# Norms of a two-block transformer kernel: 1/sqrt by a polynomial and one Newton step, VectorE's next 40 operations ordered behind it, and a ring of four for four wide weights

## The chip, the core and the metric

The kernel runs on one core of one Trainium2 chip. The metric is the device time of one execution in microseconds, as the median of several. A core has a matrix engine (TensorE, PE in the rows, with its weight load PEld), a vector engine (VectorE, DVE), an activation engine (ScalarE, ACT), a general engine (GpSimd, POOL) and a queue that starts transfers (SyncE, SP). Each engine works through its own row of instructions in a fixed order and waits where an operand is not there yet.

## What is computed

The reference is two blocks after one another over 512 tokens of width 1024. In the first, layer 0 is a mixer (chunked mLSTM beside a gated short convolution) and layer 1 grouped-query attention, with a context of 256 tokens beside; both have a squared-relu MLP. In the second, both layers add three branches (a latent attention "MLA", a differential attention with 8 heads, a memory attention), then a layer norm, an MLP and another layer norm. What matters here is where an inverse root is taken:

```python
def rms_norm(x, g):
    xf = x.astype(jnp.float32)
    y = xf * lax.rsqrt(jnp.mean(xf * xf, axis=-1, keepdims=True) + EPS)
    return (y * g.astype(jnp.float32)).astype(x.dtype)

def _layernorm(x, g, b):
    mu = jnp.mean(xf, axis=-1, keepdims=True)
    var = jnp.mean(jnp.square(xf - mu), axis=-1, keepdims=True)
    y = (xf - mu) * lax.rsqrt(var + LN_EPS) * g.astype(jnp.float32) + b.astype(jnp.float32)
    return y.astype(x.dtype)

# first block, both layers
hx = rms_norm(x, norm1_g[layer]) * (1 + mod_x[1]) + mod_x[0]
...
x = x + mod_x[5] * sqrelu_mlp(rms_norm(x, norm2_g[layer]) * (1 + mod_x[4]) + mod_x[3], mlp_w1[layer], mlp_w2[layer])
# mixer: hn = rms_norm(h, mnorm_g), attention: rms_norm of q and k by head, MLA: _rms(c_q), _rms(c_kv),
# differential attention: _rms by head of the output, second block: _layernorm after the branches and after the MLP
```

## The kernel before

**Matmuls.** Every product is taken as three: both operands are split into a high part and a remainder (`split`, L546 and L547: ScalarE casts `whi` or `Hh`, VectorE or GpSimd subtracts to get `wlo` or `Hl`), and TensorE adds high times high, high times low and low times high (L528; L531 are transposes). 512 tokens go in two parts of 256 where a norm lies between, and whole where none does.

**Weights.** They stream in one fixed order (`weight_order`) through a ring of four raw tiles, started by SyncE, and are split into rings of high and low tiles. One subtraction in three goes to GpSimd, in some stretches one in two or none. Weights of 1056 columns, which are the mixer's four `hv` pieces, have a ring of their own, `vh` and `vl`, with two tiles each. The two-tile ring is line 582.

**Norms.** The squares are summed by VectorE over the blocks of rows (`accx`, L349, for the x side), TensorE sums over the partitions with a product with ones (`colsum`), VectorE makes the variance (`var`, L737, L422 or L2139) and calls `rsqrt` (L711 to L726): a shift (L719), the well-known integer guess (L720), a product with -0.5 (L721) and three Newton steps of three operations (L723 to L725), 12 small operations on 128 x 2 to 128 x 12 numbers, of which each but one needs the one before. TensorE then spreads the result over the partitions (`bcast`, a product with the constant `cst`), and the apply step multiplies (L364). In the attention and the differential attention the result is used per head (`rq`, and `rsy` for the head outputs). There are 54 calls: 2 at the start, 6 in the mixer, 3 in the output projection of the mixer, 3 in the MLP's second product of layer 0, 2 for keys and 8 for queries in the attention, 2 in its output projection, and in each layer of the second block 2 in the MLA, 8 in the differential attention and 4 in the layer norms.

**Order.** The program is written as generators that take turns; a scheduler then fixes each engine's row from the order of emission, the dependences and its own estimate of durations. It is free to put an operation that was emitted later between two operations of an `rsqrt` chain, and does: operations such as `junk` (L636, the adaptive norms' modulations as a fused multiply and sum over a raw weight tile), `wlo`, `r` (L822, the squared relu) and the rotary steps (L1337 to L1340, with one step, `rp`, on GpSimd) stand between the chains' operations. Where the words say "a chain", they mean one `rsqrt` call's operations.

**Places named below.** In the mixer the product `px` takes its four `vh`/`vl` pieces in turn; the same stretch multiplies `Hch`, the context's high part, with `whi` into `pc`. In the output projection of the mixer each of three parts ends with four `accx` additions, `colsum` and `bcast`. In the differential attention each head transposes its probabilities `P` (L531), ScalarE casts them to `pth`, VectorE makes the remainder `ptl` (L547), and the head's next keys `dk` and queries `dq` pass the rotary steps.

## Time and profile before

| | before |
|---|---|
| median of 3 runs | 3865.19 us (3862.13 to 3867.59) |
| profiled execution | 3866.64 us |
| its span | 3864.8 us, mean granted clock 0.979 |
| TensorE busy | 3684.8 us (95%) |
| VectorE busy | 2450.4 us (63%) |
| ScalarE busy | 1560.9 us (40%) |
| GpSimd busy | 843.3 us (22%) |

The span is the time from the profile's first to its last instruction; the execution's own time is 1.8 us longer. The times of single operations below are of this execution. TensorE is busy in nearly all of it, so a time is told by where it is not busy: its waits, each with what ended it, and the stretches in which its granted clock was 0.5 and every product took twice as long.

### The profile page before, as it was taken

The page shows a single profiled execution, that of the slowest core. Times are in us where ns is not written, and L with a number is a line of the kernel's source. Part 1 is how long each engine was busy: PE and PEld are TensorE (multiplying, and loading weights), DVE is VectorE, ACT ScalarE, POOL GpSimd, SP SyncE. Part 2 cuts the span into 40 slices and gives each one's busy share as a digit, 9 for nine tenths or more (in the row PEclk, how much of TensorE's full clock was granted, in tenths as well). Part 3 has the DMA queues.
Part 4 walks back from the last instruction along what each step waited for, and adds up shares of the span by engine and source line. Part 5 has one row for each costly group of instructions (what it writes and reads, how often), then busy time and mean ns, then how long its engine had stood idle before and what let it go on. Part 6 is the DMA issues. An engine that isn't in the chain of part 4 may idle for free.

```text
span 3864.8 us, 52371 instructions
## 1 busy us (share of the span) xinstructions
PE 3684.8 (95%) x20472; PEld 3175.4 (82%) x20472; DVE 2450.4 (63%) x4615; ACT 1560.9 (40%) x2822; POOL 843.3 (22%) x550
## 2 busy tenths in 40 slices
PE   7999999999988999999999999999999999999998
PEld 7877888888878888888888778888878887788887
DVE  7577575544588784456667866544676678555445
ACT  5222432222447643335544543422365445334222
POOL 3112210000120121112222224211333222242112
PEclk8999999999989999999999999999999999999999
DMA  7322233331210133322122122222121211123331
GB/s 280 126 88 95 91 128 135 126 124 64 70 55 7 55 106 104 94 77 72 67 73 71 50 63 102 90 96 98 58 76 66 78 66 50 64 95 93 95 97 44
DMA packets 94359, 337.11 MB, mean 87 GB/s; under 512 B 10272, under 2 KB 15008, under 8 KB 93216
## 3 DMA queue, kind: packets, MB, share of 16 engines
q1 hardware_dynamic: 94112, 333.77, 25.5%
q8 instruction: 161, 2.64, 0.3%
q14 instruction: 86, 0.70, 0.1%
HBM read 326.39 MB, written 7.34 MB: 86 GB/s over the span
## 4 chain that ended last, share of the span: by engine, by line
PE 71%; DVE 11%; ACT 4%; issue 2%; POOL 2%; POOLq 0%; ACTq 0%; DVEq 0%
PE b L528 63%; PE d L528 6%; PE b L531 2%; DVE rr L1340 1%; DVE ptl L547 1%; ACT P L1315 1%; DVE wlo L547 1%; DVE nm L1307 1%; DVE rp L1337 1%; POOL mg L1681 1%; POOL rp L1339 0%; DVE dq L1599 0%; DVE rsq L723 0%; DVE qo L1599 0%; DVE rp L1338 0%
## 5 line engine op out<-in xcount | busy, mean ns | idle before, releaser
L546 ACT CAST whi<-raw 128x1024 fp32r<-128x1024 f32 (+1 forms) x349 | 363.5, 1042 | 821.7 <-PE b L528 544.0
L528 PE MATMUL b<-Hl,whi 128*128 128x512 f32 (+1 forms) x1456 | 547.2, 376 | 5.8 <-POOL Hl L547 5.0
L528 PE MATMUL b<-Hh,whi 128*128 128x512 f32 (+1 forms) x1456 | 547.5, 377 | 4.8 <-ACT Hh L546 3.5
L528 PE MATMUL b<-Hh,wlo 128*128 128x512 f32 (+1 forms) x1456 | 544.7, 375 | 0.8 <-DVE wlo L547 0.8
L547 POOL TENSOR_TENSOR wlo<-raw,whi 128x1024 fp32r<-128x1024 f32 (+1 forms) x115 | 280.4, 2438 | 1018.7 <-ACT whi L546 986.1
L547 DVE TENSOR_TENSOR wlo<-raw,whi 128x1024 fp32r<-128x1024 f32 (+1 forms) x234 | 313.6, 1340 | 217.4 <-ACT whi L546 214.6
L528 PEld LDWEIGHTS b<-Hl,whi 128*128 128x128 f32 x1456 | 276.0, 190 | 54.8 <-POOL Hl L547 8.4
L528 PEld LDWEIGHTS b<-Hh,whi 128*128 128x128 f32 x1456 | 275.4, 190 | 51.8 <-ACT Hh L546 4.4
L528 PEld LDWEIGHTS b<-Hh,wlo 128*128 128x128 f32 x1456 | 276.1, 190 | 50.3 <-DVE wlo L547 1.0
L546 ACT CAST xhi<-raw 128x1024 fp32r<-128x1024 f32 x145 | 151.7, 1049 | 391.9 <-PE b L528 383.9
L547 POOL TENSOR_TENSOR xlo<-raw,xhi 128x1024 fp32r<-128x1024 f32 x50 | 122.5, 2450 | 782.3 <-ACT xhi L546 756.1
L822 DVE TENSOR_TENSOR r<-r 128x512 f32<-128x512 f32 (+1 forms) x176 | 176.6, 1018 | 128.1 <-ACT r L821 127.9
L528 PE MATMUL b<-Hl,xhi 128*128 128x512 f32 (+1 forms) x624 | 228.6, 367 | 1.1 <-POOL Hl L547 1.0
L528 PE MATMUL b<-Hh,xhi 128*128 128x512 f32 (+1 forms) x624 | 227.0, 365 | 2.2 <-ACT Hh L546 2.2
L528 PE MATMUL b<-Hh,xlo 128*128 128x512 f32 (+1 forms) x624 | 227.1, 364 | 0.0
L636 DVE SCALAR_TENSOR_TENSOR junk<-raw,sc 128x1024 bf16<-128x1024 f32 x128 | 161.6, 1263 | 91.8 <-DMA raw<-in_wts 90.7
L531 PE MATMUL b<-cst,P 128*128 128x128 f32 x960 | 149.8, 281 | 50.8 <-DVE ptl L547 25.3
L528 PE MATMUL b<-hlx,xhi 128*128 128x512 f32 (+1 forms) x532 | 196.3, 369 | 0.0
L528 PE MATMUL b<-hhx,xlo 128*128 128x512 f32 (+1 forms) x532 | 196.2, 369 | 0.0
L528 PE MATMUL b<-hhx,xhi 128*128 128x512 f32 (+1 forms) x532 | 195.7, 368 | 0.0
L547 DVE TENSOR_TENSOR ptl<-b,pth 128x512 fp32r<-128x512 f32 (+1 forms) x272 | 165.9, 621 | 32.5 <-ACT pth L546 30.2
L528 PE MATMUL b<-hlx,whi 128*128 128x512 f32 (+1 forms) x504 | 185.8, 369 | 0.0
(669 smaller groups left out, 9726.8 us busy)
## 6 DMA issues: line engine op xcount, KB each, us to landing
raw<-in_wts SPq DMA_DIRECT2D x566, 512.0 KB, 3.4
early<-in_wts SPq DMA_DIRECT2D x16, 512.0 KB, 7.7
raw<-in_wts SPq DMA_DIRECT2D x6, 384.0 KB, 3.0
raw<-in_wts SPq DMA_DIRECT2D x4, 528.0 KB, 3.9
x<-in_xT SPq DMA_DIRECT2D x2, 1024.0 KB, 10.7
X<-in_xT SPq DMA_DIRECT2D x1, 2048.0 KB, 9.2
xd<-X SPq DMA_DIRECT2D x2, 1024.0 KB, 5.4
X<-xd SPq DMA_DIRECT2D x1, 2048.0 KB, 7.8
```

Of the source, the lines that this page charges most:

```text
L528: self.nc.tensor.matmul(out, lhsT=lhsT, rhs=rhs, start=start, stop=stop, skip_group_check=True)
L531: self.nc.tensor.transpose(out, in_, ident)
L546: nc.scalar.copy(out=hi, in_=src)
L547: (eng or nc.vector).tensor_tensor(out=lo, in0=src, in1=hi.bitcast(F32), op=ALU.subtract)
L636: nc.vector.scalar_tensor_tensor(out=junk, in0=w[:, :1024], scalar=0.5, in1=self.sc[:, v, :], op0=ALU.mult, op1=ALU.mult, accum_out=self.m ...
L822: nc.vector.tensor_tensor(out=r, in0=r, in1=r, op=ALU.mult)
L1307: nc.vector.tensor_reduce(out=nm[:, 0:1], in_=S, axis=AX.XY if len(S.shape) == 3 else AX.X, op=ALU.max, negate=True)
L1315: nc.scalar.activation(out=out, in_=S, func=AF.Exp, bias=b, scale=scale, accum_out=ssum)
L1337: nc.vector.stream_shuffle(out=t2, in_=ps, mask=mask)
L1340: nc.vector.tensor_tensor(out=dst, in0=t1, in1=t2, op=ALU.add)
L1681: nc.gpsimd.tensor_tensor(out=X[:, b, :], in0=H[0][:, b, :].bitcast(F32), in1=H[1][:, b, :].bitcast(F32), op=ALU.add)
```

## The change

`rsqrt` has 8 operations where it had 12: the guess in one operation (integer multiply by -0.5 and add of a constant), a quadratic polynomial of x = v g g in four, and one Newton step in three; all eight depend on one another in a row. `pin` then takes the next 40 VectorE operations that are emitted after a chain and gives each an order-only dependence on the chain's last operation (no semaphore), so that the scheduler cannot place them ahead of it or within it. In the layer norm the small product `lne` that follows the chain belongs to it. The mixer's wide ring has four tiles of `vh` and `vl` where it had two, and to pay for it the six row tiles of the mLSTM lie in a pool that is opened later (`rows2`).

```diff
@@ Norm.stats (layer norm)
         r = k.rsqrt(v, n)
+        k.pinned = None
         nc.vector.scalar_tensor_tensor(out=e, in0=d[:, :n], scalar=-1.0 / 1024, in1=r, op0=ALU.mult, op1=ALU.mult)
+        k.pin(True)
@@ _split
-            hi, lo = (self.t(self.wide, [P, 1152], F32R, tag=f"v{x}", bufs=2)[:, :1056] for x in "hl")
+            hi, lo = (self.t(self.wide, [P, 1152], F32R, tag=f"v{x}", bufs=4)[:, :1056] for x in "hl")
@@ rsqrt
-        nc.vector.tensor_scalar(out=i, in0=v.bitcast(I32), scalar1=1, scalar2=None, op0=ALU.logical_shift_right)
-        nc.vector.tensor_scalar(out=y.bitcast(I32), in0=i, scalar1=-1.0, scalar2=float(0x5F3759DF), op0=ALU.mult, op1=ALU.add)
-        nc.vector.tensor_scalar(out=h, in0=v, scalar1=-0.5, scalar2=None, op0=ALU.mult)
-        for _ in range(3):
-            nc.vector.tensor_tensor(out=q, in0=y, in1=y, op=ALU.mult)
-            nc.vector.tensor_tensor(out=q, in0=q, in1=h, op=ALU.mult)
-            nc.vector.scalar_tensor_tensor(out=y, in0=q, scalar=1.5, in1=y, op0=ALU.add, op1=ALU.mult)
+        self.pin(None)
+        nc.vector.tensor_scalar(out=g.bitcast(I32), in0=v.bitcast(I32), scalar1=-0.5, scalar2=float(0x5F374800), op0=ALU.mult, op1=ALU.add)
+        k, a, b = 0.37587863, -1.25284868, 1.87697019
+        r = k ** 0.5
+        nc.vector.scalar_tensor_tensor(out=q, in0=g, scalar=r, in1=g, op0=ALU.mult, op1=ALU.mult)
+        nc.vector.tensor_tensor(out=x, in0=q, in1=v, op=ALU.mult)
+        nc.vector.scalar_tensor_tensor(out=x, in0=x, scalar=a / r, in1=x, op0=ALU.add, op1=ALU.mult)
+        nc.vector.scalar_tensor_tensor(out=g, in0=x, scalar=b, in1=g, op0=ALU.add, op1=ALU.mult)
+        nc.vector.scalar_tensor_tensor(out=q, in0=g, scalar=-0.5, in1=g, op0=ALU.mult, op1=ALU.mult)
+        nc.vector.tensor_tensor(out=q, in0=q, in1=v, op=ALU.mult)
+        i = nc.vector.scalar_tensor_tensor(out=y, in0=q, scalar=1.5, in1=g, op0=ALU.add, op1=ALU.mult)
+        self.pin(i)
         return y
+    PIN = 40
+    def pin(self, ins):
+        tr = self.nc.cur_bb.bb.instructions
+        last = getattr(self, "pinned", None)
+        if last is not None:
+            a, pos = last
+            n = 0
+            for o in tr[pos:]:
+                if o.engine == a.engine and n < self.PIN:
+                    n += 1
+                    self.tc.add_manual_dep(o, a.name, mybir.DependencyInfo(mybir.DependencyClass.NoSync, mybir.DependencyReason.DATA), reason="order")
+        self.pinned = None
+        if ins is not None and self.PIN:
+            a = tr[-1]
+            self.pinned = (a, len(tr))
@@ mlstm
-        row = lambda tag: self.t(rp, [R, TA], tag=tag)
+        rq = self.pool(e_rows, "rows2")
+        row = lambda tag: self.t(rq, [R, TA], tag=tag)
```

The scheduler's rows change with it, far beyond the lines of the diff. Three places follow, each before and after. The lines of the changed kernel are shifted by 2 (split) to 27 (the branches).

ScalarE's row in the mixer, where the four wide weights `vh` are cast; `whi` are narrower weights, `q`, `k`, `va` and `ktm` copies of products. Before:

```order
L546 CAST whi_971<-raw_846 128x1024
L546 CAST vh_1089<-raw_911 128x1056
L546 CAST vh_1149<-raw_969 128x1056
L546 CAST whi_1029<-raw_864 128x1024
L1066 ACTIVATE q_893<-pc_917 128x256
L1066 ACTIVATE q_893<-px_918 128x512
L546 CAST whi_1359<-raw_1147 128x1024
```

and, ten copies of `va` and `ktm` further on:

```order
L1083 COPY ktm_896<-ms_1315 128x256
L546 CAST vh_1155<-raw_1027 128x1056
L1076 COPY va_895<-px_1319 128x2x128
L1083 COPY ktm_896<-ms_1347 128x256
L546 CAST vh_1353<-raw_1087 128x1056
L1076 COPY va_895<-px_1363 128x2x128
```

After:

```order
L548 CAST whi_963<-raw_838 128x1024
L548 CAST vh_1081<-raw_903 128x1056
L548 CAST vh_1141<-raw_961 128x1056
L548 CAST vh_1147<-raw_1019 128x1056
L548 CAST whi_1021<-raw_856 128x1024
L1092 ACTIVATE q_885<-pc_909 128x256
L1092 ACTIVATE q_885<-px_910 128x512
L548 CAST vh_1345<-raw_1079 128x1056
L548 CAST whi_1351<-raw_1139 128x1024
L1092 ACTIVATE q_885<-pc_967 128x256
```

The third cast of `vh` stands right behind the second and the fourth between two copies of q; before, they stood among the copies of `va` and `ktm`.

VectorE's row at the end of the mixer's output projection, before. `X` is the residual after its last product, `accx` the sum of squares, `hlc` and `r` belong to the context's MLP, the `rs` names to the chain:

```order
L1003 SCALAR_TENSOR_TENSOR X_3546<-b_723_4297,mods_69,X_3546 128x256
L636 SCALAR_TENSOR_TENSOR junk_4853,mods_69<-raw_4403,sc_95 128x1024
L547 TENSOR_TENSOR Hl_86<-tmp_4200,Hh_85 128x256
L349 TENSOR_TENSOR accx_3622<-accx_3622,tmp_4236 128x256
L636 SCALAR_TENSOR_TENSOR junk_4855,mods_69<-raw_4403,sc_95 128x1024
L349 TENSOR_TENSOR accx_3622<-accx_3622,tmp_4265 128x256
L822 TENSOR_TENSOR r_4446<-r_4446 128x256
L349 TENSOR_TENSOR accx_3622<-accx_3622,tmp_4294 128x256
L349 TENSOR_TENSOR accx_3622<-accx_3622,tmp_4323 128x256
L547 TENSOR_TENSOR hlc_4394<-r_4446,hhc_4393 128x256
L737 TENSOR_SCALAR var_4329<-b_725_4326 128x2
L719 TENSOR_SCALAR rsi_4331<-var_4329 128x2
```

and after:

```order
L1029 SCALAR_TENSOR_TENSOR X_3518<-d_721_4232,mods_69,X_3518 128x256
L549 TENSOR_TENSOR Hl_86<-tmp_4154,Hh_85 128x256
L549 TENSOR_TENSOR Hl_86<-tmp_4164,Hh_85 128x256
L1029 SCALAR_TENSOR_TENSOR X_3518<-b_723_4261,mods_69,X_3518 128x256
L349 TENSOR_TENSOR accx_3594<-accx_3594,tmp_4200 128x256
L349 TENSOR_TENSOR accx_3594<-accx_3594,tmp_4229 128x256
L349 TENSOR_TENSOR accx_3594<-accx_3594,tmp_4258 128x256
L349 TENSOR_TENSOR accx_3594<-accx_3594,tmp_4287 128x256
L763 TENSOR_SCALAR var_4293<-b_725_4290 128x2
L722 TENSOR_SCALAR rsg_4296<-var_4293 128x2
L725 SCALAR_TENSOR_TENSOR rsq_4297<-rsg_4296 128x2
L726 TENSOR_TENSOR rsx_4298<-rsq_4297,var_4293 128x2
```

The four additions now stand next to one another right behind the last `X`, and the two `junk` operations, `Hl` and `r` no longer among them; the eight operations of the chain follow without a break.

VectorE's row in the differential attention of the second block's first layer, at the end of the head pair's first chain, before. `ptl` from `b_3200` is the remainder of transposed probabilities, `rr` the rotary result, `dk` the next head's keys:

```order
L1338 TENSOR_TENSOR rp_3174_18655<-b_3172_18629,tab_17837 128x512
L723 TENSOR_TENSOR rsq_18583<-rsy_18581 128x4
L547 TENSOR_TENSOR wlo_18714<-raw_18418,whi_18713 128x1024
L724 TENSOR_TENSOR rsq_18583<-rsq_18583,rsh_18582 128x4
L1340 TENSOR_TENSOR rr_18654<-rp_3174_18655,rp_3175_18656 128x512
L725 SCALAR_TENSOR_TENSOR rsy_18581<-rsq_18583,rsy_18581 128x4
L1599 TENSOR_TENSOR dq_18620<-rr_18654,dq_18620 64x512 x2
L1337 STREAM_SHUFFLE rp_3182_18698<-b_3179_18671 128x512
L1338 TENSOR_TENSOR rp_3181_18697<-b_3179_18671,tab_17837 128x512
L1340 TENSOR_TENSOR rr_18696<-rp_3181_18697,rp_3182_18698 128x512
L547 TENSOR_TENSOR ptl_18758<-b_3200_18759,pth_18757 128x4x128
L2049 TENSOR_TENSOR dk_3168_18622<-rr_18696,dk_3167_18621 64x512
```

and after:

```order
L549 TENSOR_TENSOR wlo_18556<-raw_18275,whi_18555 128x1024
L549 TENSOR_TENSOR ptl_18646<-b_3200_18647,pth_18645 128x4x128
L2165 SCALAR_TENSOR_TENSOR rsum_18329<-rsum_18329 128x4
L1364 STREAM_SHUFFLE rp_3175_18544<-b_3172_18517 128x512
L1365 TENSOR_TENSOR rp_3174_18543<-b_3172_18517,tab_17729 128x512
L549 TENSOR_TENSOR wlo_18602<-raw_18310,whi_18601 128x1024
L1367 TENSOR_TENSOR rr_18542<-rp_3174_18543,rp_3175_18544 128x512
L1626 TENSOR_TENSOR dq_18508<-rr_18542,dq_18508 64x512 x2
L1364 STREAM_SHUFFLE rp_3182_18586<-b_3179_18559 128x512
L1365 TENSOR_TENSOR rp_3181_18585<-b_3179_18559,tab_17729 128x512
L2173 SCALAR_TENSOR_TENSOR ot_18431<-ot_18431,sg_17727,b_3208_18674 128x512
L1367 TENSOR_TENSOR rr_18584<-rp_3181_18585,rp_3182_18586 128x512
```

`ptl` stood behind both rotary results and now stands ahead of the first rotary step.

## Rows read from the trace of the kernel before

**Rows 1.** The page's parts 1 and 4: busy time; chain by engine

```profile
PE 3684.8 (95%) x20472; PEld 3175.4 (82%) x20472; DVE 2450.4 (63%) x4615; ACT 1560.9 (40%) x2822; POOL 843.3 (22%) x550
...
PE 71%; DVE 11%; ACT 4%; issue 2%; POOL 2%; POOLq 0%; ACTq 0%; DVEq 0%
```

**Rows 2.** TensorE's waits by releaser: us in total, times, longest

```profile
PE b L531 <- DVE ptl L547: 25.3, 11, 2.9
PE b L531 <- ACT P L1315: 18.9, 16, 6.3
PE b L528 <- DVE rsy L725: 14.5, 11, 3.8
...
PE b L528 <- DVE accx L349: 7.0, 5, 5.5
...
PE px L528 <- DVE vl L547: 4.5, 1, 4.5
```

**Rows 3.** Windows: stretch, length, busy PE, PEld, DVE, ACT, POOL, PEclk, DMA, GB/s

```profile
160.00:163.40 3.40, 3.40 (x18) 3.40 (x18) 0.10 (x2) 0.00 (x0) 0.00 (x0) 0.55 0.92 320
487.30:494.20 6.90, 5.69 (x27) 5.72 (x28) 5.18 (x18) 0.79 (x2) 0.32 (x1) 0.51 0.28 93
1100.00:1150.00 50.00, 41.05 (x198) 34.55 (x197) 46.28 (x131) 23.18 (x39) 13.34 (x7) 0.89 0.18 64
1192.00:1313.00 121.00, 111.88 (x816) 104.81 (x816) 108.85 (x217) 101.98 (x217) 7.74 (x6) 1.00 0.00 1
2057.50:2060.90 3.40, 3.37 (x9) 2.26 (x10) 2.29 (x3) 2.32 (x4) 2.69 (x2) 0.50 0.22 89
```

**Rows 4.** L719's instructions: count, ns min/median/max, first and last start

```profile
L719 DVE TENSOR_SCALAR rsi<-var x54: 150/164/2193, 31.8 to 3850.8; 128x4 int32<-128x4 int32 x27, 128x2 int32<-128x2 int32 x17, 128x8 int32<-128x8 int32 x8, 128x12 int32<-128x12 int32 x2
```

**Rows 5.** VectorE's timeline, an undisturbed chain: start us, us, operation

```profile
1045.94 0.16 DVE L719 TENSOR_SCALAR rsi<-var 128x2 int32<-128x2 int32 x1
1046.14 0.17 DVE L720 TENSOR_SCALAR rsy<-rsi 128x2 int32<-128x2 int32 x1
...
1047.91 0.16 DVE L725 SCALAR_TENSOR_TENSOR rsy<-rsq,rsy 128x2 f32<-128x2 f32 x1
```

**Rows 6.** Timeline at the mixer's wide weights, ScalarE and VectorE

```profile
153.52 1.09 ACT L546 CAST vh<-raw 128x1056 fp32r<-128x1056 f32 x1
155.37 3.45 DVE L547 TENSOR_TENSOR vl<-raw,vh 128x1056 fp32r<-128x1056 f32 x1
```

**Rows 7.** Timeline at the mixer's output projection's end, GpSimd and VectorE

```profile
482.61 2.53 POOL L547 TENSOR_TENSOR xlo<-raw,xhi 128x1024 fp32r<-128x1024 f32 x1 [1.77 <-ACT xhi L546]
482.86 2.56 DVE L822 TENSOR_TENSOR r<-r 128x256 f32<-128x256 f32 x1
485.34 3.02 DVE L349 TENSOR_TENSOR accx<-accx,tmp 128x256 f32<-128x256 f32 x2
```

**Rows 8.** Timeline at the differential attention's first chain, VectorE and TensorE

```profile
2053.24 2.83 DVE L1340 TENSOR_TENSOR rr<-rp,rp 128x512 f32<-128x512 f32 x1 [0.72 <-POOL rp L1339]
2055.99 0.68 DVE L547 TENSOR_TENSOR ptl<-b,pth 128x512 fp32r<-128x512 f32 x1
2056.72 0.44 PE L531 MATMUL b<-cst,P 128*128 128x128 f32 x2 [2.87 <-DVE ptl L547]
```

**Rows 9.** Timeline at the MLP's second part, TensorE and VectorE

```profile
1025.75 0.58 PE L528 MATMUL b<-ones,accx 128*128 128x1 f32 x4 [0.48 <-DVE accx L349]
1026.56 0.17 DVE L719 TENSOR_SCALAR rsi<-var 128x2 int32<-128x2 int32 x1
1029.07 2.19 DVE L724 TENSOR_TENSOR rsq<-rsq,rsh 128x2 f32<-128x2 f32 x1
1031.61 0.57 PE L528 MATMUL b<-cst,rsy 128*128 128x128 f32 x3 [2.19 <-DVE rsy L725]
```

**Rows 10.** VectorE's timeline in the attention's first heads

```profile
1136.57 0.16 DVE L723 TENSOR_TENSOR rsq<-rq 128x8 f32<-128x8 f32 x1
1136.65 0.16 DVE L719 TENSOR_SCALAR rsi<-var 128x8 int32<-128x8 int32 x1
```

5 lines of the change are left out of this document (3 added, 2 removed).

## Prediction

> **What bounds the kernel now.** I read the page's busy times first: TensorE is busy for 3684.8 of the span's 3864.8 us, VectorE for 63% of it, and the chain of work that ended last runs through TensorE for 71% and VectorE for 11% [rows 1]. So a faster VectorE operation is worth something only where TensorE stands still for it, or runs at half clock behind such a stand. TensorE's waits by releaser come next: the remainder `ptl` of transposed probabilities (25.3 us in 11 waits), the attention's probabilities `P` (18.9), the chains' result `rsy` (14.5 in 11), the sums `accx` (7.0, of which one is 5.5) and one wait of 4.5 us for `vl` [rows 2]. Third, windows behind the long waits: the 3.40 us from 160 had a clock of 0.55, the 6.9 us from 487.3 had 0.51, the 3.40 us from 2057.5 had 0.50 [rows 3]. At half of full speed (1.2 for 2.4 GHz) a stretch of 3.4 us loses 1.7, one of 6.8 us 3.4. Short waits do not do this: from 1192 to 1313 TensorE was idle for 9 of 121 us, in single waits, and its clock was 1.00 [rows 3].
>
> **The fewer operations.** 54 chains lose 4 of 12 operations each. One takes 0.164 us at the median [rows 4], so VectorE is busy for 54 x 4 x 0.164 = 35 us less. Nearly none of that is TensorE's. What it can be is the length of a chain that TensorE waits for: undisturbed, dependent operations start 0.20 us after one another ((1047.91 - 1046.14) / 9), and twelve took 2.13 us [rows 5]. Eight, all dependent, take 7 x 0.20 + 0.16 = 1.56, or 0.57 less. Where others stand between them, an operation costs less: two neighbours from different chains started 0.08 us apart [rows 10]. So twelve spread ones cost VectorE about 1.0 us, and eight in one piece 1.56.
>
> The Trainium skill ("VectorE: DVE Perf Modes", "The DRAIN you can't avoid" and "Rules for kernel authors") says that the next operation doesn't start until the pipe has emptied, and that a chain is made faster by fewer operations, not by fewer waits. Here the rows agree only for dependent ones [rows 5]; the 0.08 us between independent ones [rows 10] speaks against it, so I count with the rows. The rival below counts the other way.
>
> **The ring of four.** The third `vh` cast came at 153.52, among the copies of `va`, because a ring tile came free only then; its subtraction ran on VectorE from 155.37 for 3.45 us [rows 6], and TensorE stood for 4.5 us [rows 2], then ran 3.4 us at half clock (1.7). The new order has this cast right behind the second, long before. All of it gone would be -6.2. Two casts and two subtractions move ahead, against whatever stands there, up to the 3.45 us of one subtraction. I take -5, between -6.2 and -2.
>
> **The output projection's end.** TensorE waited 5.5 us for `accx` [rows 2]. Ahead of the last two additions stood two `junk` operations and `r`, which took 2.56 us because GpSimd's `xlo` ran until 485.14, and then the pair of additions took 3.02 in the same way [rows 7]. The new order has the four additions side by side right behind the last `X`, which is what `pin` does to `r` and the `junk` emitted later. Four additions cost about 4 x 0.4; the 5.5 us and the 3.4 of half clock make 8.9. A quarter of the loss comes back if an addition falls behind a GpSimd operation (2.5 us). I take -6.5, between -8.9 and -3. Behind the chain stand now `wlo`, `r` and `junk`; for `wlo` waits TensorE, and that is counted with the parts.
>
> **The differential attention.** At 2056.72 TensorE waited 2.87 us for `ptl`, which stood on VectorE behind a rotary addition of 2.83 us, itself held by GpSimd [rows 8]. With the chain in one piece the scheduler puts that `ptl` ahead of both rotary steps. Four of the eleven waits have this shape, two in each layer; the mean wait is 25.3 / 11 = 2.3 us, and each is followed by 3.4 us at half clock (1.7). All of it would be 4 x 4.0 = -16. But the next thing that TensorE needs is `dk`, which hangs on the same late rotary addition, and only the transposed block's products, 12 to 15 of 0.12 us, stand between. So the wait may keep much of its length under another name. I take -7 (all the clock at two of the four places, half of the wait at all), between -16 and 0.
>
> **The other chains that TensorE waits for.** The scheduler reckons with a shorter chain and so puts the `bcast` nearer. In the three parts of the projection, the three of the MLP's second product and the two of the attention's output, 13 or 14 products of 256 columns (0.12 us each, 1.6 us) stand between `colsum` and `bcast`, where there were 15 to 52. What is needed: `colsum` began at 1025.75, the chain 0.81 later, and 1.56 + about 0.15 follow to the `bcast` [rows 9, 5]; less `colsum`'s own 0.44 that is 2.1. So eight parts get a wait of about 0.4, +3.4, or at most 0.95 each, +7.6. Against that, in the before, chain operations fell behind GpSimd's subtractions: one took 2.19 us and TensorE waited 2.19 us for the result [rows 9]. A shorter window in one piece catches fewer of these; of 14.5 us I take 5 back, at most 12. Sum -1.5, between -9 and +7.
>
> **The attention's first heads.** VectorE is the bound here: busy for 46.28 of 50 us [rows 3]. Eight query chains in one piece cost 1.56 where they cost about 1.0 spread out, +4.5, less the operations that they made wait. Also the softmax's maximum `nm` now stands behind a chain, and `P`, for which TensorE waits 18.9 us [rows 2], starts later by up to one chain. I take +3, between -4 and +8.
>
> **The rest.** Six chains in the mixer are no longer torn apart by others, the layer norms' chains neither, and the last chain of the kernel, with nothing behind it that hides it, loses up to 0.57. Moved `junk` releases its raw tile at other times, which may delay a weight's loading; no such wait is among those of [rows 2]. I take -1, between -5 and +5. The row tiles that move to a later pool are written by the same operations as before; if that delays the mLSTM's start, it is within the bound of +5.
>
> **Sum**, against the execution's own 3866.64 (span 3864.8 and 1.84 around it): -5 - 6.5 - 7 - 1.5 + 3 - 1 = -18.0, so 3848.6. This execution lay 1.45 above the median of the runs, so 3847.2 against 3865.19.
>
> **Rivals.**
> *A, slower: the order holds up what TensorE needs.* 54 times, 40 operations may not go ahead of a chain that itself waits for `colsum`. If a pinned `wlo` or `nm` is late at the eight parts and each of these waits (0.95 us and the `wlo` behind it) is long enough to halve the clock (1.7), that is 8 x 2.65 = +21, and +8 in the attention; against it stand -5 and -6.5 and the rest, -3: 3866.6 + 14.5, less 1.45, gives 3879.7. It decides at whether a wait below 1 us halves the clock. The window from 1192 with its 1.00 speaks against it; VectorE at 46.28 of 50 us speaks for the part in the attention.
> *B, no change: only ring and projection are real.* The `ptl` wait becomes a `dk` wait of the same length, the parts get 0.95 each and give nothing back: -5 - 6.5 + 7.6 + 3 - 1 = -1.9, 3863.3. For it: `dk` hangs on the same addition. Against it: the products that now stand between.
> *C, faster still: each operation taken out counts in full.* Where VectorE is the bound, 4 x 0.164 us go at each of eight query chains, -5.2 where I have +3: 3839. That is what the skill's rule would make of it, as said above. Against it: the 0.08 us between neighbours.
>
> **How the numbers follow.** Forecast 0.52, C 0.12, B 0.22, A 0.14. 0.2% (7.7 us), about what a measurement of this kernel can tell from no change, puts faster below 3857.5 and slower above 3872.9. The forecast's low edge, with the bounds not all at one end, is some 15 lower (3832) and its high edge some 12 higher (3859), of which 0.04 lie above 3857.5. Faster: 0.52 + 0.12 - 0.04 + 0.04 (part of B's edge) = 0.64; same 0.24, since B spreads to both sides; slower 0.12, as A, priced at its full size, ends within 0.2% in a part of its cases. The range goes from 3831 to 3866, which leaves out A and the low tail.
>
> **What would show it.** The `vl` wait is gone and the clock at 160 is 1.00; `accx` waits sum to under 2 us and the clock from 487 is 1.00 (ring and projection right). The `ptl` waits at the first chains of both layers are under 1 us, without 3.4 us at half clock behind them; waits for `dk` of 2 us there mean that B is right. `rsy` waits: more than eleven, shorter, none above 1.5 us. A heads' period at 1100 to 1150 that is longer than before, or half clock behind waits of 0.4 to 1 us, means A; shorter by more than 0.5 us each, C. The prediction is wrong altogether if the scheduler's new rows make a new wait of several us at a place not named here, such as for a weight's `wlo` behind a chain.

## The result, and the profile after

The changed kernel takes 3898.16 us (median of 4 runs, 3895.43 to 3901.22), the kernel before 3863.83 beside it (4 runs, 3862.13 to 3867.59): a ratio of 1.009 (95% interval 1.0077 to 1.0102). It is slower by 34 us, where 18 us faster were forecast. The profiled execution took 3896.01 with a span of 3893.9, against 3866.64 and 3864.8 before.

The page's part 1 of the changed kernel (engine, busy time, share of the span, instructions):

```profile
PE 3693.5 (95%) x20472; PEld 3176.4 (82%) x20472; DVE 2438.9 (63%) x4399; ACT 1560.6 (40%) x2822; POOL 847.7 (22%) x550
```

Against [rows 1], VectorE has 216 instructions fewer (54 x 4) and is busy for 11.5 us less, not 35. It is the order that keeps the rest: without it, in e1 and e12 below, VectorE is busy for 2414.1 and 2412.3 us, 36 and 38 less than before. TensorE does the same 20472 matmuls. The gaps between the first and the last of them sum to 182.9 us in place of 162.4 (+20.5), and in that time it runs at half clock (1.2 GHz) for 172.2 us in place of 156.1; half of the difference, 8.1 us, is time lost. Together that is 28.6 of the 29.1 us by which the span grew. So the change costs waits of TensorE and the half clock behind them, and nothing else that shows.

TensorE's waits by releaser, in the changed kernel (us in total, times, longest):

```profile
PE b L533 <- ACT P L1342: 20.9, 20, 9.2
PE b L530 <- DVE ptl L549: 14.5, 10, 3.3
PE b L533 <- DVE ptl L549: 12.8, 7, 4.2
...
PE b L530 <- DVE rsy L731: 8.4, 6, 3.4
PE pc L530 <- ACT whi L548: 7.5, 2, 6.3
PE b L530 <- DVE wlo L549: 7.3, 4, 4.2
PE b L530 <- DVE accx L349: 6.8, 5, 2.8
...
PE b L530 <- ACT dk L2074: 6.1, 6, 2.1
```

Beside [rows 2]: the `vl` wait is gone; `rsy` fell from 14.5 to 8.4; the `ptl` wait before the product with `P` (the row with L533) halved, but 14.5 us before other products stand in its place, with 6.1 for `dk`. `P` now waits up to 9.2. New are the waits for weights: 6.3 for `whi` and 4.2 for `wlo`.

**Where it went.** All kernels issue the same matmuls, and in nearly the same order, so the k-th matmul of one trace can be laid against the k-th of the other. (The scheduler exchanges neighbours: in the changed kernel 3917 of the 20472 places hold another product than before. Counted from the start to each border of the table, at most ten matmuls differ in shape, so the terms by stage stand.) The table shows how much later (+) or earlier each stage ends in each run's profile, less what the stages ahead already brought; the stages are named with their times in the kernel before. The runs other than "after" are told below.

| run | to 210 | mixer 210-415 | projection 415-516 | MLP 516-1091 | attention 1091-1396 | MLP, MLA 1396-2041 | diff. 2041-2293 | norms, MLP 2293-2830 | MLA 2830-3082 | diff. 3082-3333 | end | sum |
|---|---|---|---|---|---|---|---|---|---|---|---|---|
| after | -7.1 | **+17.6** | -4.9 | +2.1 | +6.6 | **+6.5** | **+9.7** | -4.1 | **+6.5** | +1.6 | -5.5 | +29.1 |
| e1_no_order | -4.9 | +0.6 | -3.4 | -1.7 | +6.3 | +0.4 | +0.4 | -4.8 | +1.2 | -3.3 | -8.1 | -17.2 |
| e2_ring_only | -3.9 | +0.3 | +0.4 | 0 | -0.1 | 0 | 0 | 0 | +0.1 | -0.1 | 0 | -3.4 |
| e3_old_chain | -1.3 | +22.3 | -4.9 | -1.3 | +15.4 | +8.5 | +16.7 | -1.5 | +6.8 | +7.4 | -1.2 | +66.9 |
| e4_no_order_mixer | -5.8 | +0.3 | -5.7 | +0.3 | +9.7 | +6.5 | +15.2 | -3.2 | +6.6 | +1.8 | -5.5 | +20.1 |
| e5_junk_free | -5.6 | +2.2 | -5.2 | +0.8 | +10.6 | +8.7 | +9.6 | -4.1 | +6.5 | +1.7 | -7.5 | +17.8 |
| e7_order_8 | -5.6 | +4.2 | -3.8 | -4.9 | +9.8 | +9.8 | +21.2 | -4.3 | +7.0 | +2.6 | -6.9 | +29.1 |
| e8_weights_free | -7.5 | +6.4 | -1.9 | -2.1 | +10.2 | -0.1 | +18.0 | -8.3 | +1.3 | +7.1 | -11.4 | +11.7 |
| e9_rotary_free | -5.3 | +6.2 | -1.9 | +0.5 | +9.8 | -1.3 | +10.2 | -8.3 | +1.2 | +6.3 | -12.0 | +5.5 |
| e10_softmax_free | -6.6 | +6.2 | -3.2 | -0.7 | +8.6 | -1.3 | +10.2 | -8.4 | +1.2 | +6.4 | -12.4 | +0.2 |
| e14_gate_free | -5.5 | +1.2 | -3.7 | +0.8 | +4.5 | +0.3 | +4.3 | -7.3 | +3.1 | -3.1 | -12.4 | -17.8 |
| e12_chain_only | -2.8 | +0.1 | -3.9 | -0.8 | +5.3 | -0.8 | +3.0 | -5.2 | +1.2 | -3.4 | -8.1 | -15.2 |
| e13_no_order_diff | -6.6 | +17.7 | -4.9 | +2.0 | +6.4 | +5.4 | 0.0 | -2.4 | +6.2 | -3.7 | -6.0 | +14.1 |
| e6_hout_only | -4.2 | +2.9 | -5.3 | -6.2 | +6.5 | +0.3 | +0.2 | -4.7 | +1.3 | -3.4 | -8.1 | -20.7 |
| e11_hout_late_queries | -3.2 | +0.6 | -4.9 | -4.6 | +3.5 | -0.8 | +2.9 | -5.1 | +1.4 | -3.5 | -8.1 | -21.9 |

Each row is one profiled execution, and some of these terms hold up to 5 us that no edit made (the last section). Windows of the changed kernel (stretch, length, busy PE, PEld, DVE, ACT, POOL, clock, DMA share, GB/s), at the mixer's wide weights, in the mixer's later part and at the projection's end:

```profile
155.00:163.00 8.00, 8.00 (x68) 8.00 (x67) 0.69 (x6) 1.12 (x3) 0.00 (x0) 1.00 0.01 2
318.00:331.00 13.00, 4.60 (x26) 3.63 (x25) 9.51 (x23) 3.19 (x10) 2.66 (x2) 0.81 0.24 80
485.00:515.00 30.00, 28.74 (x234) 27.99 (x233) 26.88 (x55) 18.63 (x45) 12.50 (x10) 1.00 0.30 106
```

The first and the last show two of the forecast gains: where [rows 3] had a clock of 0.55 and 0.51, the clock is 1.00 and TensorE is busy for 8.00 of 8 and 28.74 of 30 us. The second is the largest loss: 13 us in which TensorE works for 4.6. The kernel before, same view and same stretch, has 13.00 busy there:

```profile
318.00:331.00 13.00, 13.00 (x77) 10.46 (x75) 9.84 (x31) 4.35 (x13) 2.46 (x2) 1.00 0.24 83
```

The timeline of the changed kernel tells why (start, us, engine, line, operation, output and inputs; in brackets the idle time before it and who ended it):

```profile
301.09 1.23 DVE L638 SCALAR_TENSOR_TENSOR junk<-raw,sc 128x1024 bf16<-128x1024 f32 x1
...
319.41 0.17 DVE L763 TENSOR_SCALAR var<-ss 128x4 f32<-128x4 f32 x1 [1.77 <-ACT sqj L1257]
321.00 0.16 DVE L731 SCALAR_TENSOR_TENSOR rsy<-rsq,rsg 128x4 f32<-128x4 f32 x1
321.08 1.22 DVE L638 SCALAR_TENSOR_TENSOR junk<-raw,sc 128x1024 bf16<-128x1024 f32 x1
...
329.08 1.05 ACT L548 CAST whi<-raw 128x1024 fp32r<-128x1024 f32 x1 [7.28 <-DMA raw<-in_wts]
...
330.18 0.58 PE L530 MATMUL pc<-Hch,whi 128*128 128x256 f32 x1 [6.28 <-ACT whi L548]
```

Between 301.09 and 321.08 no `junk` starts, though VectorE is idle meanwhile, the last time for 1.77 us until the chain's input comes. The chain runs, and only then eleven `junk` follow until 339. (With `junk` alone untied, as in e5 below, seven of them run in that stretch.) `junk` is the last reader of a raw weight tile, of which four rotate: while it is held, the next weight isn't loaded. In the trace SyncE starts no load between 307.3 and 325.8 us; in e5 it starts three, at 309.0, 313.4 and 321.1. So ScalarE waits 7.28 us for the load of `raw`, and TensorE 6.28 us for its cast. The prediction named this in its term "the rest", without a price of its own.

### The profile page after: what moved, and what is told of

It reads as the page before. It is cut to its first block, busy times and chain, and to the rows that moved or that the text cites. A ratio compares the mean times of both kernels' runs of the same rounds, so it can differ in the third digit from the quotient of the medians.

```text
span 3893.9 us, 52256 instructions
## 1 busy us (share of the span) xinstructions
PE 3693.5 (95%) x20472; PEld 3176.4 (82%) x20472; DVE 2438.9 (63%) x4399; ACT 1560.6 (40%) x2822; POOL 847.7 (22%) x550
## 3 DMA queue, kind: packets, MB, share of 16 engines
q1 hardware_dynamic: 94112, 333.77, 25.4%
## 5 line engine op out<-in xcount | busy, mean ns | idle before, releaser
L549 DVE TENSOR_TENSOR wlo<-raw,whi 128x1024 fp32r<-128x1024 f32 (+1 forms) x234 | 321.1, 1374 | 189.6 <-ACT whi L548 186.2
L638 DVE SCALAR_TENSOR_TENSOR junk<-raw,sc 128x1024 bf16<-128x1024 f32 x128 | 169.5, 1324 | 69.7 <-DMA raw<-in_wts 67.8
L533 PE MATMUL b<-cst,P 128*128 128x128 f32 x960 | 154.5, 279 | 39.7 <-ACT P L1342 20.9
L530 PE MATMUL b<-hhx,wlo 128*128 128x512 f32 (+1 forms) x504 | 185.9, 369 | 0.0
```

The lines of the kernel that those rows point to most:

```text
L530: self.nc.tensor.matmul(out, lhsT=lhsT, rhs=rhs, start=start, stop=stop, skip_group_check=True)
L533: self.nc.tensor.transpose(out, in_, ident)
L549: (eng or nc.vector).tensor_tensor(out=lo, in0=src, in1=hi.bitcast(F32), op=ALU.subtract)
L638: nc.vector.scalar_tensor_tensor(out=junk, in0=w[:, :1024], scalar=0.5, in1=self.sc[:, v, :], op0=ALU.mult, op1=ALU.mult, accum_out=self.m ...
```

## The experiments

All runs compute the whole kernel. The theory after the result: the order (the tying of the next 40 operations) is what costs, the shorter chain and the ring gain; it costs because independent operations that feed a load, a weight or another engine are held behind a chain that itself waits. The rivals: the chain itself costs it, or the ring with its moved row tiles. Then, place by place, the question is which held operation it is. Ratios are to the kernel before on the same chip, with 95% intervals; the medians of before were 3866.42, 3866.01, 3869.61 and 3867.97 for the four groups (e1 to e4, e5 to e8, e9 to e12, e13 and e14).

| run | median, us | ratio | interval |
|---|---|---|---|
| e1_no_order | 3848.42 | 0.9955 | 0.9941-0.9970 |
| e2_ring_only | 3864.44 | 0.9996 | 0.9987-1.0006 |
| e3_old_chain | 3930.81 | 1.0167 | 1.0151-1.0182 |
| e4_no_order_mixer | 3885.27 | 1.0044 | 1.0029-1.0058 |
| e5_junk_free | 3882.13 | 1.0045 | 1.0030-1.0060 |
| e6_hout_only | 3845.43 | 0.9950 | 0.9935-0.9965 |
| e7_order_8 | 3895.55 | 1.0078 | 1.0063-1.0093 |
| e8_weights_free | 3880.42 | 1.0037 | 1.0026-1.0048 |
| e9_rotary_free | 3870.62 | 0.9998 | 0.9989-1.0008 |
| e10_softmax_free | 3867.10 | 0.9999 | 0.9989-1.0008 |
| e11_hout_late_queries | 3844.17 | 0.9935 | 0.9918-0.9952 |
| e12_chain_only | 3850.18 | 0.9947 | 0.9932-0.9961 |
| e13_no_order_diff | 3883.67 | 1.0045 | 1.0028-1.0062 |
| e14_gate_free | 3850.56 | 0.9960 | 0.9944-0.9976 |

**The three parts apart.** First the changed kernel without the order:

```diff
-    PIN = 40
+    PIN = 0
```

> The changed kernel without the order: the chain of 8 operations and the ring of four stay, no VectorE operation is tied behind a chain. Theory 1 (the order is what costs: operations tied behind a chain hold up loads and weights' remainders): the 34 us go and some of the forecast gains stay, 3840 to 3862. Theory 2 (the shorter chain is what costs, since the scheduler puts the broadcast too near): it stays slow, 3885 to 3900. Theory 3 (the ring of four costs in the mixer): 3880 to 3895, with the 6 us wait for a weight at 330 still there.

3848.42: 18 us faster than before. The order costs 34 + 18 = 52 us of the changed kernel. Next the kernel before with the ring and the row tiles' pool alone:

```diff
-            hi, lo = (self.t(self.wide, [P, 1152], F32R, tag=f"v{x}", bufs=2)[:, :1056] for x in "hl")
+            hi, lo = (self.t(self.wide, [P, 1152], F32R, tag=f"v{x}", bufs=4)[:, :1056] for x in "hl")
...
-        row = lambda tag: self.t(rp, [R, TA], tag=tag)
+        rq = self.pool(e_rows, "rows2")
+        row = lambda tag: self.t(rq, [R, TA], tag=tag)
```

> The kernel before with the ring of four and the row tiles' later pool alone. Theory 1: the ring's gain of 7 us by 180 stays to the end, 3853 to 3860. Theory 3: the early wide weights use up the loads that the mixer's end needs, a wait of several us for a weight near 330, 3870 to 3885. Theory 2 says nothing against 3853 to 3860.

The `vl` wait is gone and the trace is 3.9 us ahead at 210, but the time can't be told from that of before. It lies between the two forecasts and bears out neither; slower it is not, so the ring is not the culprit. Then the old chain of twelve inside the changed kernel, with order and ring:

```diff
         self.pin(None)
-        nc.vector.tensor_scalar(out=g.bitcast(I32), in0=v.bitcast(I32), scalar1=-0.5, scalar2=float(0x5F374800), op0=ALU.mult, op1=ALU.add)
...
+        nc.vector.tensor_scalar(out=i, in0=v.bitcast(I32), scalar1=1, scalar2=None, op0=ALU.logical_shift_right)
...
+        for _ in range(3):
...
-        self.pin(i)
+        self.pin(ins)
```

> The changed kernel with the old chain of 12 operations, tied in the same way (40 operations behind it), and the ring. Theory 1: as slow as the changed kernel or slower by up to 54 times a fraction of 0.57 us, 3895 to 3915. Theory 2: near the kernel before, 3855 to 3875.

3930.81, 64 us above before and slower than expected: behind a longer chain the order costs more, not less. And the new chain alone, without order and ring:

```diff
-            hi, lo = (self.t(self.wide, [P, 1152], F32R, tag=f"v{x}", bufs=4)[:, :1056] for x in "hl")
+            hi, lo = (self.t(self.wide, [P, 1152], F32R, tag=f"v{x}", bufs=2)[:, :1056] for x in "hl")
...
-    PIN = 40
+    PIN = 0
...
-        rq = self.pool(e_rows, "rows2")
-        row = lambda tag: self.t(rq, [R, TA], tag=tag)
+        row = lambda tag: self.t(rp, [R, TA], tag=tag)
```

> The kernel before with the chain of 8 operations alone: ring of two, no order. The difference of the runs without order and with the ring alone says -16 for the chain (3864.4 to 3848.4): 3846 to 3856 if the parts add up. If the chain's gain needs the ring, 3858 to 3866.

19 us faster than before. So the chain brings all of what e1 gained, the ring nothing that shows in the end, and the order takes back more than twice that.

**The mixer.** The order left out behind the mixer's six chains alone:

```diff
             r = self.rsqrt(self.meanvar(ss, 4, 128, 1e-6), 4)
+            self.pinned = None
```

> The changed kernel without the order behind the mixer's six chains alone. Theory 1: the stretch from 300 to 400, which lost 22 us against the kernel before, loses under 5, so 3874 to 3884, and the rest of the loss (attention 7, MLA 6, differential attention of the first layer 11) stays. Theory 3: the wait for a weight near 330 stays and so does the time, 3890 to 3900.

Against after, the mixer's +17.6 becomes +0.3 and the time 15 us less (each kernel less its own before: 18.9 for 34.3), 1.3 us above theory 1's range. What among the 40 does it? Here the `junk` operations alone are not tied, in the whole kernel:

```diff
+    free = set()
...
             nc.vector.scalar_tensor_tensor(out=junk, in0=w[:, :1024], scalar=0.5, in1=self.sc[:, v, :], op0=ALU.mult, op1=ALU.mult, accum_out=self.mods[:, L, v, j:j + 1])
+            self.free.add(self.nc.cur_bb.bb.instructions[-1].name)
...
                     n += 1
+                    if o.name in self.free:
+                        continue
```

> The changed kernel, but the modulations' operations (junk) are not tied behind a chain; all others of the 40 are, as before. Theory 1a (in the mixer the tied junk operations hold raw tiles, so weights load late): the wait of 6 us for a weight near 330 is gone, and the stretch from 300 to 400 loses under 6 against the kernel before instead of 22, so 3876 to 3888 in all. Theory 1b (in the mixer the cost is that the chain's tied operations of the mLSTM come late, not the loads): it stays 3893 to 3902.

It gives the same: 16.1 us above before, the mixer at +2.2, and the gaps between TensorE's matmuls in the mixer back from 24.3 us to the 11.5 of before. The same window as above, of this run:

```profile
318.00:331.00 13.00, 11.82 (x67) 9.62 (x66) 8.29 (x23) 4.46 (x12) 1.86 (x1) 1.00 0.29 88
```

TensorE is busy for 11.82 us where it was for 4.60. The mechanism in the mixer, held `junk` and late loads, is settled.

**Fewer operations tied.** With 8 in place of 40:

```diff
-    PIN = 40
+    PIN = 8
```

> The changed kernel with 8 operations tied behind each chain instead of 40. Theory 1 (cost by the operations that are held): between the kernel without order (3848) and the changed one (3898), 3855 to 3885. If the chain in one piece is itself what costs, not what is held behind it, it stays near 3898.

The expectation failed: 3895.55, as slow as 40 within the interval. The mixer lost only 4.2, but the first differential attention 21.2. A few operations right behind the chain are enough to do as much harm, at other places; the number that is tied doesn't set the price.

**Weights and transposed probabilities.** Besides `junk`, a weight's `wlo` and the remainder `ptl` are not tied:

```diff
         self.split(hi[:, :kb * c], lo[:, :kb * c], src, eng=eng)
+        self.free.add(self.nc.cur_bb.bb.instructions[-1].name)
...
         self.split(hi, lo, ps[:, :n * P].rearrange("p (a b) -> p a b", a=n))
+        self.free.add(self.nc.cur_bb.bb.instructions[-1].name)
```

> The changed kernel, but junk, the weights' remainders (wlo and its kin) and the transposed probabilities' remainders (ptl) are not tied; everything else of the 40 is. Theory 1 with these as the ones that TensorE and the loads wait for: most of the 50 us between order and no order go, 3848 to 3868; in the MLA of the first layer the 4 us wait for wlo is gone and the differential attention of the first layer loses under 4 instead of 11. If it stays above 3880, what is held and costs is something else (nm, the rotary steps, the residual).

Against after the time fell by 20 of the 52 us that the order costs, and 18 of these came with `junk` alone (e5). In the part of the latent attention's projections (MLA) the +6.5 became -0.1, in the second layer +1.3. The changed kernel's timeline there, VectorE with one row of GpSimd:

```profile
1792.23 2.35 POOL L549 TENSOR_TENSOR wlo<-raw,whi 128x1024 fp32r<-128x1024 f32 x1
...
1789.36 0.69 DVE L1367 TENSOR_TENSOR qp<-rp,rp 128x512 f32<-128x512 f32 x1 [0.83 <-POOL rp L1366]
...
1791.32 0.97 DVE L725 SCALAR_TENSOR_TENSOR rsq<-rsg 128x4 f32<-128x4 f32 x1
1792.30 2.82 DVE L1367 TENSOR_TENSOR qp<-rp,rp 128x512 f32<-128x512 f32 x1
1795.05 0.15 DVE L726 TENSOR_TENSOR rsx<-rsq,var 128x4 f32<-128x4 f32 x1
...
1796.10 2.09 DVE L549 TENSOR_TENSOR wlo<-raw,whi 128x768 fp32r<-128x768 f32 x2
...
1797.10 0.62 PE L530 MATMUL b<-cH,wlo 128*128 128x512 f32 x1 [4.21 <-DVE wlo L549]
```

and that of the kernel before, the same `wlo` and its product:

```profile
1776.39 0.95 DVE L547 TENSOR_TENSOR wlo<-raw,whi 128x768 fp32r<-128x768 f32 x1
...
1777.39 0.50 PE L528 MATMUL b<-cH,wlo 128*128 128x512 f32 x1 [0.55 <-DVE wlo L547]
```

The order holds only what was written behind the chain. The rotary addition `qp` was written ahead of it and stands in its midst; it takes 2.82 us, where the same operation three microseconds before took 0.69, because GpSimd's `wlo` began 0.07 us earlier. That an operation of VectorE with two inputs in SBUF is held for the whole of a GpSimd operation that started first and reads SBUF is what the Trainium skill says ("SBUF — State Buffer", "SBUF: two separate sides": the port pair shared by GpSimd and VectorE is an exclusive lock); the 2.82 beside the 2.35 agrees. VectorE's own `wlo` waits for the whole chain, and TensorE 4.21 us for a `wlo`; in the kernel before, that one stood inside the chain, ahead of the held `qp`, and TensorE waited 0.55. But the time fell by only 1.7 against e5, which can't be told from none: the differential attention rose from +9.6 to +18.0 and from +1.7 to +7.1, the mixer by 4.2. That the scheduler sets other rows elsewhere for what is freed at one place would explain the first two; the mixer's 4.2 is of the kind that no edit made (half clock for 13.7 us from 298.5, as in the last section).

**Rotary steps, softmax.** The three VectorE operations of a rotation are freed too, and then also the softmax's maximum `nm` and its scaling:

```diff
         nc.vector.stream_shuffle(out=t2, in_=ps, mask=mask)
+        self.free.add(self.nc.cur_bb.bb.instructions[-1].name)
         nc.vector.tensor_tensor(out=t1, in0=ps, in1=cos, op=ALU.mult)
+        self.free.add(self.nc.cur_bb.bb.instructions[-1].name)
...
         nc.vector.tensor_tensor(out=dst, in0=t1, in1=t2, op=ALU.add)
+        self.free.add(self.nc.cur_bb.bb.instructions[-1].name)
```

> As the run before with junk, wlo and ptl not tied, and the three VectorE operations of each rotary step not tied either. If the differential attention's remaining loss (waits of 2.8 us for dk behind the first chains, about 13 us in the first layer) comes from rotary steps held behind the chain, it goes to under 4 and the whole to 3862 to 3874; if it comes from the chain's place or the other operations, it stays 3877 to 3885.

```diff
         nc.vector.tensor_reduce(out=nm[:, 0:1], in_=S, axis=AX.XY if len(S.shape) == 3 else AX.X, op=ALU.max, negate=True)
+        self.free.add(self.nc.cur_bb.bb.instructions[-1].name)
...
                 nc.vector.tensor_tensor(out=nm[:, 1:2], in0=b, in1=scale, op=ALU.mult)
+                self.free.add(self.nc.cur_bb.bb.instructions[-1].name)
```

> As that, and the softmax's maximum and its scaling (nm) not tied either. If the attention's first heads lose their 8 to 10 us because nm, and so P, is held behind the query chains, this loss goes to under 3, and with the rotary steps the whole is 3850 to 3865. If nm is late for another reason (the chain in one piece on a full VectorE), the attention loses 8 as before.

Freeing the rotation took the first differential attention from +18.0 to +10.2, not to under 4, and the time to that of before. Freeing `nm` moved the time by nothing that can be measured: 3867.10 is above the expected range, and the attention as a whole still has +8.6. But the trace shows its place. The changed kernel at the attention's first heads, VectorE and TensorE:

```profile
1145.24 0.17 DVE L731 SCALAR_TENSOR_TENSOR rq<-rsq,rsg 128x8 f32<-128x8 f32 x1
1145.33 0.95 DVE L1334 TENSOR_REDUCE nm<-d 128x1 f32<-128x768 f32 x1
1147.32 0.15 DVE L1340 TENSOR_TENSOR nm<-nm,rq 128x1 f32<-128x1 f32 x1
1148.71 1.54 PE L533 MATMUL b<-cst,P 128*128 128x128 f32 x6 [9.16 <-ACT P L1342]
```

and with `nm` free, the same product:

```profile
1131.81 1.54 PE L533 MATMUL b<-cst,P 128*128 128x128 f32 x6 [5.86 <-ACT P L1350]
```

The maximum of a score that is ready stands behind a query chain; its wait for `P` was 6.3 us before [rows 2], is 9.16 with the order and 5.86 with `nm` free. Over the matmuls of the first heads (6400 to 6820) the shift is +7.1 in the changed kernel, +6.5 in e9 and -0.9 in e10; without the order it is -2.0 (e1, e12). The loop of heads behind them gives it back (below): +7.4 in e10.

**The differential attention.** The order left out behind its chains alone:

```diff
             on[h].append(self.rsqrt(v, 4))
+            self.pinned = None
```

> The changed kernel without the order behind the differential attention's chains alone (both layers). If the order's cost there is the order's own, the 11 us that the first layer lost and the 4 of the second are gone, with the mixer's, the attention's and the MLA's losses left: 3880 to 3888. If the differential attention runs worse because the scheduler entered it in another state (a stage ahead had changed), it loses about as much as with the order: 3893 to 3900.

The two layers go from +9.7 and +1.6 to 0.0 and -3.7, and the time is 18.6 us less than after's (each less its before), of which these two stages explain 15. Which operation? `ptl`, `wlo`, rotation and `nm` are not tied in e10, so what these stages lose there is not theirs. In e10's trace the gate's product `gt` of the heads before was left behind the chain, so it was freed as well:

```diff
                 nc.vector.scalar_tensor_tensor(out=ts[i], in0=ts[i], scalar=1.0, in1=o, op0=ALU.add, op1=ALU.mult)
+                self.free.add(self.nc.cur_bb.bb.instructions[-1].name)
```

> As the run with the softmax's operations also not tied, and the gates' product (gt) not tied either. If the 10 us that the first layer's differential attention still loses there come from gt held behind the chain (the next projections of q and k then stand later in TensorE's row), the loss falls under 4 and the whole to 3853 to 3862; if not, it stays 3862 to 3872.

17.4 us below before, which is faster than expected, and 15 us below e10; the first layer's loss is +4.3. In the two differential attentions the gaps between matmuls went from 22.8 and 22.6 us to 18.0 and 15.1 (before: 15.9 and 15.6). VectorE's timeline in e10, with the first product of the next pair's `dq` on TensorE:

```profile
2047.44 1.28 DVE L1982 SCALAR_TENSOR_TENSOR gt<-gt,b 128x512 f32<-128x512 f32 x2
...
2048.27 0.49 PE L530 MATMUL b<-Hh,whi 128*128 128x512 f32 x1
...
2054.06 0.01 DVE L1373 LOAD_MASK_SELECT rp<-b  x1 [4.74 <-PE b L530]
```

and in e14:

```profile
2036.97 0.39 PE L530 MATMUL b<-Hh,whi 128*128 128x512 f32 x1
...
2037.68 0.68 DVE L1982 SCALAR_TENSOR_TENSOR gt<-gt,b 128x512 f32<-128x512 f32 x1
...
2042.64 0.01 DVE L1373 LOAD_MASK_SELECT rp<-b  x1
```

In e10 both `gt` stand behind the chain and the product starts only behind the first of them. In e14 the first `gt` ran at 2025.04, long before the chain, and the second within it. The product starts 11.3 us earlier and the next pair's rotation 11.4 us, without VectorE's 4.74 us of waiting for TensorE's product. Of these, 6.3 us are a lead that e14 had before any row differs (the last section); some 5 us are the edit's. This row of e10's list of TensorE's waits, for ScalarE's `dk`, shrinks to 0.5 us in e14's:

```profile
PE b L530 <- ACT dk L2086: 10.4, 4, 2.8
```

That the held `gt` keeps a PSUM bank which that product needs is read from the code, which gives both the same tag; no run has tried another bank. With six kinds of operations untied, e14 is as fast as the kernel without any order.

**The order only where it was forecast to help.** Behind the three chains of the mixer's output projection, and nowhere else:

```diff
     PIN = 40
+    tie = False
...
-        if ins is not None and self.PIN:
+        if ins is not None and self.PIN and self.tie:
...
+        self.tie = True
         self.proj8("hout", [(k, k) for k in (4, 5, 6, 7, 0, 1, 2, 3)], Stream.act, S, parts, pp, evac, rms.finish)
+        self.tie = False
```

> The chain of 8 operations and the ring of four everywhere, the order only behind the three chains of the mixer's output projection. Without any order the projection lost 1 us against the kernel before, with it it gained 6; if places are independent of one another, this is 5 us below the kernel without order, 3841 to 3846 (theory 1). If the order changes what the scheduler does far away, it can be anything from 3835 to 3875.

and behind the last query chains of the attention too:

```diff
+                    self.tie = True
                     qstat(b)
+                    self.tie = False
```

> The order behind the projection's three chains (3845 alone) and behind the last two query chains of the attention. Without order the attention's steady loop ran at 21.4 us for two heads against 20.2 before, and lost 7.5 us; with the order everywhere it ran at 20.0 but its start lost 7. If the loop's state is set by its last two chains and the start's loss by the six ahead, 3836 to 3842; if both come from the last two, 3843 to 3852.

3845.43 and 3844.17: both beat both kernels, by 20.6 and 25.4 us against before. From e1's -18.0 and from each other they can't be told (0.9935 lies in e6's interval). In the trace, the projection's part is -5.3 and -4.9 against e1's -3.4. So e6 falls into its narrow range, but that the order adds anything there isn't shown by the time. The second's time lies in the range for both coming from the last two chains. It also asked after a loss that isn't the order's: in the steady loop of the attention the matmuls of two heads (137, of which a record may be missing) took, in the kernel before, in e1 and in the changed kernel, windows as above:

```profile
1212.40:1232.50 20.10, 18.59 (x136) 17.44 (x136) 18.09 (x37) 16.98 (x37) 1.29 (x1) 1.00 0.00 1
```

```profile
1202.20:1223.70 21.50, 19.56 (x137) 17.52 (x137) 17.91 (x37) 17.07 (x37) 1.29 (x1) 1.00 0.00 1
```

```profile
1227.00:1247.00 20.00, 18.83 (x137) 17.30 (x137) 17.76 (x37) 16.89 (x36) 1.29 (x1) 1.00 0.00 1
```

The matmuls are the same, and VectorE, ScalarE and GpSimd are busy for no longer in e1, yet the loop takes 1.4 us longer each time, +7.5 us in all between 1212 and 1331. e12 has it as well, so it comes with the new chain, not with the ring. e11 takes most of it away (+1.5), but the attention as a whole went only from +6.3 to +3.5. Why the loop finds one phase or the other stays open.

## Why the prediction was wrong, point by point

**The sum came out for another kernel.** 3847.2 was forecast; without the order the time is 3848.42. That is luck: the sum's 18 us were to come from the ring, the projection and the differential attention, while e12 gains 19 by the shorter chain alone, most of it in the layer norms (-5.2), at the kernel's end (-8.1) and in the projection (-3.9). The step that failed is the price of the order. The sum had it as a maker of gains (projection, differential attention) and as a loss of 3 in the attention; it costs 52 us. The prediction looked at operations that the chain had torn apart and asked what their new place brings; it didn't ask, for each of the up to 40 operations tied behind each of 54 chains, who waits for it. Held `junk` holds loads, held `wlo` holds a product, held `nm` the softmax, held `gt` the next pair's projection.

**The ring, -5: right** in its stretch. No wait for `vl`, clock 1.00 at 160, -3.9 with the ring alone at 210, within the bounds. No gain of it shows in the whole time (0.9996).

**The projection's end, -6.5: right in size, the reason only in part,** -4.9, within the bounds. The four additions stand together; VectorE's and TensorE's timeline:

```profile
489.84 2.00 DVE L349 TENSOR_TENSOR accx<-accx,tmp 128x256 f32<-128x256 f32 x4
491.99 0.58 PE L530 MATMUL b<-ones,accx 128*128 128x1 f32 x4 [0.19 <-DVE accx L349]
495.61 0.68 PE L530 MATMUL b<-cst,rsy 128*128 128x128 f32 x4 [0.51 <-DVE rsy L731]
```

The wait of 5.5 [rows 2] is 0.19, and the `bcast` waits 0.51 where about 0.4 was reckoned. But e1 and e12 have -3.4 and -3.9 there without the order, and the four additions stand together in them too, so it isn't `pin` that brings them together. In e12:

```profile
478.77 2.00 DVE L349 TENSOR_TENSOR accx<-accx,tmp 128x256 f32<-128x256 f32 x4
```

Most of this gain comes with the shorter chain. The order takes the wait for `accx` there from 2.4 us to 0.19, and the stage gains 1 to 2. The `accx` waits of the whole kernel sum to 6.8, not to under 2: others came up in the MLP (3.7) and later.

**The differential attention, -7: wrong in sign,** +9.7 and +1.6. (Its own terms, half of four waits of 2.3 us and 3.4 us of clock, make 8.0 and not 7; nothing hangs on it.) The first step held: the `ptl` wait before `P` went from 25.3 in 11 to 12.8 in 7. The next one failed, as rival B feared: other products wait for `ptl` (14.5 in 10) and `dk` (6.1). And the `ptl` wait wasn't what decides: e14 has 24.8 us of it again, in 18 waits,

```profile
PE b L533 <- DVE ptl L549: 24.8, 18, 2.7
```

and yet is 5.9 and 9.5 us better in these two stages than e10 with its 13.2. No run gains anything in the first of them; the best in the second is -3.7.

**The other chains, -1.5: about right where no weight is held.** `rsy` fell from 14.5 in 11 to 8.4 in 6, more than the 5 taken. The sign for it failed: more than eleven short waits were foretold, none above 1.5 us, and there are six, one of 3.4. The MLP came to +2.1. What wasn't in this term is `wlo` behind the chain in the two MLA parts, of whose 13 us together e8 took back 12. The prediction's last sentence named it as what would make all wrong.

**The attention, +3: right in kind, too small.** +6.6; the first heads alone have +7.1, of which `P` has 2.9 in one wait (9.16 for 6.26). Without the order they gain 2.0, so the order costs 9 there. That e1 and e12 lose 6.3 and 5.3 in the whole attention is the loop behind them (+7.5).

**The rest, -1: wrong twice.** In the mixer the loss was 17.6 where +5 was the bound, some 15 of it by `junk` (e5); and the chain's length gained 8.1 at the kernel's end and about 5 in the layer norms' stage (e1, e12), where up to 0.57 a chain was taken at one place only. Why a chain that is 0.57 us shorter can gain more than that, the first chain of the last stretch shows, GpSimd and VectorE in the kernel before:

```profile
3338.73 2.34 POOL L547 TENSOR_TENSOR wlo<-raw,whi 128x1024 fp32r<-128x1024 f32 x1 [26.63 <-ACT whi L546]
3338.88 2.20 DVE L725 SCALAR_TENSOR_TENSOR rsy<-rsq,rsy 128x4 f32<-128x4 f32 x1
```

and in e12:

```profile
3331.60 2.39 POOL L549 TENSOR_TENSOR wlo<-raw,whi 128x1024 fp32r<-128x1024 f32 x1 [26.61 <-ACT whi L548]
3331.16 0.16 DVE L731 SCALAR_TENSOR_TENSOR rsy<-rsq,rsg 128x4 f32<-128x4 f32 x1
```

Before, the chain's last operation fell 0.15 us behind the start of a subtraction on GpSimd and took 2.20 us, and TensorE waited 2.15 for it. The shorter chain ends 0.28 us ahead of that subtraction, and the wait is gone. The second place is an `lne` of 2.30 us (TensorE waited 1.89), which takes 0.16 in e12. In the whole kernel 24 operations of chains took over 0.4 us before, 15 do in e12 and e1, and 8 in the changed kernel. The prediction had this mechanism in its term on the other chains, for 5 us of gain; the order does make it rarer still, at a higher price elsewhere.

**The rivals.** A had the right mechanism and the wrong price. It asked whether a wait below 1 us halves the clock; what came were waits of 2 to 9 us at places that hold loads and weights. C, each operation taken out counts in full at the query chains: too much; with the chain alone the first heads came to -2.0, where C had -5.2, and with the order to +7.1. The Trainium skill, whose rule C followed, says in the same place ("VectorE: DVE Perf Modes", "The DRAIN you can't avoid") that a next operation which isn't held starts earlier, and the 0.08 us of [rows 10] agrees with that.

## What to carry to other kernels

An order that keeps a chain in one piece holds everything that is tied behind it until the chain's last input has come, also what is ready and has nothing to do with it: go through the tied operations by who waits for each (a tile to be loaded again, a bank, a weight, the next engine), leave those free, and tie only where the trace shows a chain torn apart with TensorE waiting at its end. Few tied operations are no safer than many. When a change has several parts, price each one alone: here the shorter chain was worth 19 us, and the order next to it, meant to help it, cost 52. And look for what runs beside a chain on an engine that can hold it: ending 0.28 us ahead of such an operation, in place of running into it, was worth 2 us to TensorE.
